# Gate and up products by Strassen's scheme, the down product over all PSUM banks, and a rearranged mixer order, in a fused encoder block

## The chip, the cores and the metric

One core of a Trainium2 chip runs the whole program. The metric is device time in microseconds of one execution, and the figure of a kernel is the median of its runs. TensorE (PE) multiplies, VectorE (DVE), ScalarE (ACT) and GpSimd (POOL) do the elementwise work, and SyncE (SP) issues nearly all transfers.

## What is computed

The block works on 512 tokens of 1024 channels in float32: a SwiGLU layer, a mixer, and a second SwiGLU layer, each with a norm ahead and a norm and a residual behind.

```python
def swiglu(x, w_gu, w_down):
    gu = x @ w_gu
    gate, up = gu[..., :D_FF], gu[..., D_FF:]
    return (jax.nn.silu(gate) * up) @ w_down

    f = swiglu(rmsnorm(x, ffn1_norm_pre), ffn1_w_gu, ffn1_w_down)
    x = x + 0.5 * rmsnorm(f, ffn1_norm_post)
    m = hybrid_mixer(rmsnorm(x, mix_norm_pre), ...)
    x = x + rmsnorm(m, mix_norm_post)
    f = swiglu(rmsnorm(x, ffn2_norm_pre), ffn2_w_gu, ffn2_w_down)
    x = x + 0.5 * rmsnorm(f, ffn2_norm_post)
```

D_FF is 2816, that is 22 blocks of 128. The mixer has a recurrence over 8 heads (solved here in chunks by small matrix products) and a causal convolution of width 31, both fed by one projection, and a shared output projection.

## The kernel before

**Three products for one.** Every large product is made from operands that are split in two: a high part, rounded to the type fp32r, and a low part, the rest. `mm3` (L118 to 125) issues three matmuls for each 128x128 block of weights: high by high, low by high, high by low. A block of weights, [128, 1024] float32 and 512 KB, is loaded by SP into a raw buffer (`wload`), cast on ACT into its high part (L97) and subtracted on DVE into its low part (L100), in `wblock`. The pool for these holds two raw, two high and two low buffers.

**Order of the work.** An engine works through its instructions in order. The order is fixed when the program is built: the framework walks the program with modelled times and, at each engine, lets the ready instruction go first that has the lowest priority number. Numbers follow the order of the program text; `tc.cur_priority` shifts them, and `after` forces one instruction behind another. The loads of `load` (L74) are chained, so they keep their order in SP's queue, and one that waits for a buffer holds those behind it. `PLAN`, a string, sets the order of the mixer's steps and how far some are put off; the `T_` strings say which PSUM tags a step uses. PSUM has eight banks, here three of tag A, three of B and two of C (D is C as well).

**An FFN** (`ffn`). `token_halves` makes the first four blocks of weights (gate and up of f = 0 and 1) on 256 tokens at a time, because the second half of the tokens is still being normed and turned (`Turn`: transposes on PE, split on ACT and DVE, L171 and L172, or L176 and L178 in the first FFN). Then f runs from 2 to 21: two blocks of weights, gate and up, each with 8 slices of the contraction, three matmuls of 512 tokens for each slice, 48 matmuls for an f. Then `tail`: silu on ACT (L294), product with up on DVE (L295), and the split of the result (L297, L298). The down product goes over the outputs in two halves of 512 columns: half 0 for k from 0 to 21, half 1 for k to 13 in the same manner, and the last eight k token block by token block, so that each of the four token blocks ends early and its norm (`Post.piece`, L244; `rs`; `add`, L251) and the next layer's norm and transposes (`between`) run beside the matmuls of the next block. `Post.piece` of half 0 runs ahead of that, for all four blocks.

**Between the stages.** The first three blocks of the mixer's projection (`LEAD`) are cast during the end of FFN 1 and go through `token_halves` as well. `w_out` makes the mixer's output projection in the same way, with `ahead` in it: it loads and casts the first four blocks of FFN 2 and loads the residual (`x2`, four tiles, from the DRAM copy `xs`). In that stage the raw weights lie in the tag "g", which has 22 buffers of 4 KB a partition. FFN 1 keeps its input `x` in SBUF until the end of its down product, and so does FFN 2 with `x2`.

## Time and profile before

| | |
|---|---|
| median of 3 runs | 1077.54 us (1077.13 to 1078.13) |
| the profiled execution's own time | 1079.54 us |
| its span, from first to last instruction | 1077.3 us |
| mean granted clock of TensorE | 0.977 |
| DMA moved | 101.27 MB, 94 GB/s |

The profile is of one execution. A duration in it is that of one instruction on its engine, and on one engine the next instruction may start before the one before it has ended, so the distance between two starts is what a busy engine takes for each. For TensorE the starts of successive matmuls are used throughout. "Idle before" is the time in which the engine stood, with what ended it behind the arrow.

### The profile page before, as it was taken

Reading aid. Unit: us, or ns where it says so; the run is one execution under the profiler, and the core shown is the slowest. Engines: PE = TensorE matmul, PEld = TensorE weight load, DVE = VectorE, ACT = ScalarE, POOL = GpSimd, SP = SyncE. Lnnn points to the kernel's source line nnn. Section 1 sums busy time; section 2 is a strip of 40 time slices with the busy share of each in tenths; the row PEclk is TensorE's granted clock in tenths of the full one; section 3 lists DMA queues with packets and bytes.
Section 4 is the critical chain, followed back from the end, with each engine's and each line's share of the span. In section 5 each row is a group of like instructions: output and inputs, shape, how many; then the busy total and the mean of one; then the engine's idle time right before and its main releaser. Section 6 shows DMA issues by size and latency. Waiting matters only on the chain.

```text
span 1077.3 us, 15404 instructions
## 1 busy us (share of the span) xinstructions
PE 1029.7 (96%) x6274; PEld 847.1 (79%) x6274; DVE 532.2 (49%) x1011; ACT 406.7 (38%) x628; POOL 151.1 (14%) x170
## 2 busy tenths in 40 slices
...
GB/s 235 64 93 99 97 98 98 98 99 98 98 98 221 52 92 60 50 80 60 89 90 21 114 81 37 162 20 85 106 84 101 94 99 97 98 98 98 98 117 78
DMA packets 52846, 101.27 MB, mean 94 GB/s; under 512 B 28584, under 2 KB 28712, under 8 KB 52776
## 3 DMA queue, kind: packets, MB, share of 16 engines
...
q10 hardware_dynamic: 864, 2.63, 0.7%
...
## 4 chain that ended last, share of the span: by engine, by line
PE 78%; DVE 11%; ACT 3%; POOL 3%; DMA 2%; issue 2%; SPq 1%; DVEq 0%; ACTq 0%
PE ps L125 25%; PE ps L121 25%; PE ps L124 25%; POOL cacc L521 3%; DVE ps L513 2%; DVE x L251 1%; ACT ms_j L132 1%; PE ps L652 1%; DVE wlo L100 1%; DVE rs_w L50 1%; DMA N<-md 1%; DVE fg L244 1%; PE ps L618 0%; ACT whi L97 0%; ACT cpr L520 0%
## 5 line engine op out<-in xcount | busy, mean ns | idle before, releaser
L121 PE MATMUL ps<-hT,whi 128*128 128x512 f32 (+1 forms) x888 | 340.3, 384 | 2.7 <-ACT hT L171 2.6
L124 PE MATMUL ps<-hT,wlo 128*128 128x512 f32 (+1 forms) x888 | 339.0, 382 | 0.7 <-DVE wlo L100 0.7
L125 PE MATMUL ps<-hT,whi 128*128 128x512 f32 (+1 forms) x888 | 338.4, 382 | 1.2 <-DVE hT L172 1.0
L100 DVE TENSOR_TENSOR wlo<-wraw,whi 128x1024 fp32r<-128x1024 f32 x141 | 175.3, 1244 | 313.9 <-ACT whi L97 313.7
L97 ACT CAST whi<-wraw 128x1024 fp32r<-128x1024 f32 x141 | 147.5, 1047 | 288.9 <-PE ps L125 168.3
L121 PEld LDWEIGHTS ps<-hT,whi 128*128 128x128 f32 x888 | 169.0, 190 | 38.7 <-ACT hT L171 3.6
L125 PEld LDWEIGHTS ps<-hT,whi 128*128 128x128 f32 x888 | 168.7, 190 | 38.1 <-issue 4.8
L124 PEld LDWEIGHTS ps<-hT,wlo 128*128 128x128 f32 x888 | 168.8, 190 | 34.0 <-DVE wlo L100 1.3
L521 POOL TENSOR_TENSOR cacc<-cacc,cpr 128x192 f32<-128x192 f32 (+2 forms) x120 | 118.5, 988 | 51.9 <-ACT cpr L520 43.7
L121 PE MATMUL ps<-whi,g 128*128 128x512 f32 x288 | 112.0, 389 | 0.0
L124 PE MATMUL ps<-whi,g 128*128 128x512 f32 x288 | 112.0, 389 | 0.0
L125 PE MATMUL ps<-wlo,g 128*128 128x512 f32 x288 | 104.4, 389 | 0.0
L294 ACT ACTIVATE sg<-ps 128x512 f32<-128x512 f32 x44 | 26.3, 598 | 166.1 <-PE ps L125 166.1
L295 DVE TENSOR_TENSOR sg<-sg,ps 128x512 f32<-128x512 f32 x44 | 30.3, 688 | 111.6 <-PE ps L125 111.6
L520 ACT ACTIVATE cpr<-gpad,vecs 128x192 f32<-128x192 f32 (+2 forms) x120 | 67.6, 574 | 36.4 <-POOL cacc L521 36.0
L154 POOL TENSOR_TENSOR fg<-x,gain 128x1024 f32<-128x1024 f32 x8 | 19.1, 2385 | 441.1 <-DVE x L251 436.5
L124 PEld LDWEIGHTS ps<-whi,g 128*128 128x128 f32 x288 | 54.1, 188 | 11.3
L125 PEld LDWEIGHTS ps<-wlo,g 128*128 128x128 f32 x288 | 54.1, 188 | 11.2
L121 PEld LDWEIGHTS ps<-whi,g 128*128 128x128 f32 x288 | 54.1, 188 | 11.1
L513 DVE SCALAR_TENSOR_TENSOR ps<-gpad,vecs,ps 128x320 f32<-128x320 f32 (+1 forms) x87 | 40.3, 464 | 1.4
L298 DVE TENSOR_TENSOR g<-sg,g 128x512 fp32r<-128x512 f32 x44 | 30.1, 685 | 1.4 <-ACT g L297 1.4
L297 ACT CAST g<-sg 128x512 fp32r<-128x512 f32 x44 | 27.0, 613 | 5.5 <-DVE sg L295 5.5
...
## 6 DMA issues: line engine op xcount, KB each, us to landing
wraw<-w SPq DMA_DIRECT2D x145, 512.0 KB, 3.6
lraw<-w SPq DMA_DIRECT2D x17, 512.0 KB, 5.1
gain<-gains ACTq DMA_DIRECT2D x5, 512.0 KB, 4.6
x<-x SPq DMA_DIRECT2D x4, 512.0 KB, 6.5
xs<-x SPq DMA_DIRECT2D x4, 512.0 KB, 2.7
x<-xs SPq DMA_DIRECT2D x4, 512.0 KB, 6.4
out<-x SPq DMA_DIRECT2D x3, 512.0 KB, 2.6
...
```

The source lines that it names most:

```text
L97: c.last_hi = nc.scalar.copy(hi, raw)
L100: c.last_lo = nc.vector.tensor_tensor(lo, raw, hi, ALU.subtract)
L121: i = nc.tensor.matmul(out, lhsT=lh, rhs=rh, start=start, stop=False)
L124: nc.tensor.matmul(out, lhsT=ll, rhs=rh, start=False, stop=False)
L125: return nc.tensor.matmul(out, lhsT=lh, rhs=rl, start=False, stop=stop)
L294: nc.scalar.activation(sg, psg, AF.Silu)
L295: nc.vector.tensor_tensor(sg, sg, psu, ALU.mult)
L297: nc.scalar.copy(g[:, 0], sg)
L298: nc.vector.tensor_tensor(g[:, 1], sg, g[:, 0], ALU.subtract)
L513: self.dve_queue(nc.vector.scalar_tensor_tensor(dst, gp[:, j : j + n], dw[:, j : j + 1], lo, ALU.mult, ALU.add), False)
L520: nc.scalar.mul(pr, gp[:, n + j : j + SEQ], dw[:, j : j + 1])
L521: self.pool_queue(nc.gpsimd.tensor_tensor(hi, hi, pr, ALU.add), j == 1)
```

## The change

- **Units.** f = 0 to 3 stay as they were. The other 18 are made in 18 `Unit`s to an FFN, by turns two gate blocks and two up blocks. A unit's product is a 2 by 2 matrix of blocks: two blocks of 128 output features, two halves of the contraction, two halves of the tokens. Strassen's scheme (in Winograd's form) makes it with seven block products instead of eight, and sums ahead of and behind them. Each product has 4 slices, three matmuls of 256 tokens each: 84 matmuls for a unit.
- **Sums ahead.** Of the weights: four sums of 512 columns on DVE, and high and low parts of 3.5 times 1024 columns (`wblock`, `dh`/`dl`, `sh`/`sl`, `a22`). Of the activations: `Combos`, once for each FFN, 14 instructions of 1024 columns on DVE and four casts on ACT, placed in the program behind f = 1 and ahead of f = 2.
- **Sums behind.** In `run`: one copy on ACT, five additions on DVE that read PSUM. Silu and product work on 1024 columns at a time.
- **Down.** `ffn_down` takes a block of 128 rows and all 1024 columns for each k, into eight accumulators in all eight banks; the last four k go token block by token block. The split of the gated product moves here. `Post.piece` of both halves runs in the token loop.
- **Buffers.** Tags with fixed counts (`SLOTS`) replace the 22 buffers of "g" and the separate pool for `x` and the gains. `sums` and `dif` have one buffer each, the sums' high and low parts one each, a22 one, the differences two. The input is loaded again during the down product; FFN 2's is first stored to `xs2`. The raw weights of `w_out` and of FFN 2's first four blocks share the two buffers of "raw2".
- **Mixer.** `PLAN`, three priority offsets (`O_PV`, `O_N`, `O_T`) and three PSUM tag strings get new values.

```diff
@@ -77,11 +77,19 @@
...
+SLOTS = {"g": 12, "s34": 4, "s12": 2, "sr": 2, "a22": 1, "sg": 2, "tmp": 2, "raw2": 2}
...
+def slot(c, shape, dt, name, tag="g"):
+    return c.gp.tile(shape, dt, name=name, tag=tag, bufs=SLOTS[tag])
@@ -271,78 +279,214 @@
...
-def preload(c, blocks, tag, raws=(), own=2, prev=None, aprev=None):
+def preload(c, blocks, tag, raws=(), own=2, prev=None, aprev=None, home="g"):
...
     for n, i in enumerate(blocks):
         hi = lo = None
         if n >= own:
-            hi = c.gp.tile([P, 1024], F32R, name="lhi", tag="g", bufs=NF)
-            lo = c.gp.tile([P, 1024], F32R, name="llo", tag="g", bufs=NF)
+            hi, lo = (slot(c, [P, 1024], F32R, name, h) for name, h in zip(("lhi", "llo"), home if len(home) == 2 else (home, home)))
         ws.append(wblock(c, i, hi, lo, raws[n] if n < len(raws) else wload(c, i, tag), prev, aprev))
     return ws
...
-def ffn(c, wbase, ws, turn, gpost, scale, finish, ahead=None):
+class Combos:
+    def __init__(self, c, ht, pool, tag):
+        nc = c.nc
+        self.ht = ht
+        self.t = pool.tile([P, 4, 2, KD // 2, 256], F32R, name="tsum", tag=tag)
+        q = lambda s, kh, th: ht[:, s, kh * 4 : kh * 4 + 4, th * 256 : th * 256 + 256]
+        d = slot(c, [P, 4, 256], F32, "td")
+        e = slot(c, [P, 4, 256], F32, "te")
+        T = slot(c, [P, 4, 256], F32, "ts")
+        def keep(n, x):
+            nc.scalar.copy(self.t[:, n, 0], x)
+            nc.vector.tensor_tensor(self.t[:, n, 1], x, self.t[:, n, 0], ALU.subtract)
+        sub = lambda o, a, b: nc.vector.tensor_tensor(o, a, b, ALU.subtract)
+        add = lambda o, a, b: nc.vector.tensor_tensor(o, a, b, ALU.add)
+        sub(d, q(0, 1, 1), q(0, 0, 1))
+        sub(e, q(1, 1, 1), q(1, 0, 1))
+        add(d, d, e)
+        keep(2, d)
+        sub(T, q(0, 0, 1), q(0, 0, 0))
+        sub(e, q(1, 0, 1), q(1, 0, 0))
+        add(T, T, e)
+        keep(0, T)
+        d = slot(c, [P, 4, 256], F32, "td")
+        sub(d, q(0, 1, 1), T)
+        add(d, d, q(1, 1, 1))
+        keep(1, d)
+        e = slot(c, [P, 4, 256], F32, "te")
+        sub(e, q(0, 1, 0), d)
+        add(e, e, q(1, 1, 0))
+        keep(3, e)
+    def t_(self, n):
+        return lambda s, k: self.t[:, n, s, k]
+    def b(self, kh, th):
+        return lambda s, k: self.ht[:, s, kh * 4 + k, th * 256 : th * 256 + 256]
+class Unit:
+    def __init__(self, c, i, cb, aprev=None):
+        self.c, self.cb = c, cb
+        nc = c.nc
+        r0, r1 = wload(c, i), wload(c, i + 1, "raw2")
+        H = slice(0, 512), slice(512, 1024)
+        sums = slot(c, [P, 1024], F32, "s12", "sr")
+        dif = slot(c, [P, 1024], F32, "s34", "sr")
+        S1, S2, S3, S4 = sums[:, H[0]], sums[:, H[1]], dif[:, H[0]], dif[:, H[1]]
+        add_eng = nc.gpsimd if POOL_ADDS else nc.vector
+        add_eng.tensor_tensor(S1, r1[:, H[0]], r1[:, H[1]], ALU.add)
+        add_eng.tensor_tensor(S3, r0[:, H[0]], r1[:, H[0]], ALU.subtract)
+        wh, wl = wblock(c, i, raw=r0, aprev=aprev)
+        nc.vector.tensor_tensor(S2, S1, r0[:, H[0]], ALU.subtract)
+        nc.vector.tensor_tensor(S4, r0[:, H[1]], S2, ALU.subtract)
+        dh, dl = slot(c, [P, 1024], F32R, "dhi", "s34"), slot(c, [P, 1024], F32R, "dlo", "s34")
+        a22 = slot(c, [P, 2, 512], F32R, "a22", "a22")
+        sh, sl = slot(c, [P, 1024], F32R, "shi", "s12"), slot(c, [P, 1024], F32R, "slo", "s12")
+        nc.scalar.copy(dh, dif)
+        nc.vector.tensor_tensor(dl, dif, dh, ALU.subtract)
+        nc.scalar.copy(sh, sums)
+        nc.vector.tensor_tensor(sl, sums, sh, ALU.subtract)
+        nc.scalar.copy(a22[:, 0], r1[:, H[1]])
+        c.last_hi = c.last_hi
+        nc.vector.tensor_tensor(a22[:, 1], r1[:, H[1]], a22[:, 0], ALU.subtract)
+        self.w = {"a11": (wh[:, H[0]], wl[:, H[0]]), "a12": (wh[:, H[1]], wl[:, H[1]]), "a22": (a22[:, 0], a22[:, 1]),
+                  "s1": (sh[:, H[0]], sl[:, H[0]]), "s2": (sh[:, H[1]], sl[:, H[1]]),
+                  "s3": (dh[:, H[0]], dl[:, H[0]]), "s4": (dh[:, H[1]], dl[:, H[1]])}
+    def mm(self, out, w, x):
+        h, l = self.w[w]
+        for k in range(4):
+            ks = slice(k * P, k * P + P)
+            mm3(self.c, out, h[:, ks], l[:, ks], x(0, k), x(1, k), k == 0, k == 3)
+    def run(self, n):
+        c, nc, cb = self.c, self.c.nc, self.cb
+        tt = nc.vector.tensor_tensor
+        pa, pb, pc, pd = (psum(c, [P, 2, 256], T_UNIT[n % 2][j]) for j in range(4))
+        u = slot(c, [P, 4, 256], F32, "u", "tmp")
+        self.mm(pa[:, 0], "a11", cb.b(0, 0))
+        self.mm(pa[:, 1], "s2", cb.t_(1))
+        nc.scalar.copy(u[:, 3], pa[:, 0])
+        tt(u[:, 0], u[:, 3], pa[:, 1], ALU.add)
+        self.mm(pb[:, 0], "s1", cb.t_(0))
+        self.mm(pb[:, 1], "s3", cb.t_(2))
+        tt(u[:, 1:3], u[:, 0:1].broadcast_to([P, 2, 256]), pb, ALU.add)
+        self.mm(pd[:, 0], "a12", cb.b(1, 0))
+        tt(u[:, 0], u[:, 3], pd[:, 0], ALU.add)
+        tt(u[:, 3], u[:, 2], pb[:, 0], ALU.add)
+        self.mm(pc[:, 0], "s4", cb.b(1, 1))
+        self.mm(pc[:, 1], "a22", cb.t_(3))
+        tt(u[:, 1:3], u[:, 1:3], pc, ALU.add)
+        return u
+T_UNIT = ("ABAC", "ABAD")
+POOL_ADDS = False
...
+def ffn_up(c, wbase, ws, turn, pool, tag):
     nc = c.nc
...
+    gs = []
+    def pair():
+        g = slot(c, [P, 2, 512], F32, "g2")
+        gs.extend([g[:, 0], g[:, 1]])
+        return g
+    pss = [psum(c, [P, 512], tag) for tag in "AAAD"]
+    token_halves(c, ws, pss, turn)
+    for f0 in range(0, LEADF, 2):
+        g = pair()
+        sg = slot(c, [P, 2, 512], F32, "sg", "sg")
...
+            if f0 == 0:
+                ps = pss[2 * f : 2 * f + 2]
+            else:
+                ps = []
+                for j in range(2):
+                    wh, wl = wblock(c, wbase + 2 * (f0 + f) + j, aprev=turn.last if f0 + f == 2 else None)
+                    ps.append(psum(c, [P, 512], "A"))
+                    for k in range(KD):
+                        mm3(c, ps[j], wh[:, k * P : k * P + P], wl[:, k * P : k * P + P], turn.ht[:, 0, k], turn.ht[:, 1, k], k == 0, k == KD - 1)
+            nc.scalar.activation(sg[:, f], ps[0], AF.Silu)
+            nc.vector.tensor_tensor(g[:, f], sg[:, f], ps[1], ALU.mult)
+        if f0 == LEADF - 4 or LEADF == 2:
+            cb = Combos(c, turn.ht, pool, tag)
+    for n in range(NF - LEADF):
+        un = Unit(c, wbase + 2 * LEADF + 2 * n, cb, aprev=turn.last if n == 0 and LEADF == 2 else None)
+        u = un.run(n)
+        if n % 2 == 0:
+            sg = slot(c, [P, 4, 256], F32, "sg", "sg")
+            nc.scalar.activation(sg, u, AF.Silu)
+        else:
+            g = pair()
+            nc.vector.tensor_tensor(g.rearrange("p a (h t) -> p (a h) t", h=2), sg, u, ALU.mult)
+    return gs
...
+NS = 4
+LEADF = 4
...
+def ffn_down(c, wbase, gs, gpost, scale, finish, xin, ahead=None):
+    nc = c.nc
+    wd = wbase + 2 * NF
+    acc = [[psum(c, [P, 512], t) for t in tt] for tt in T_DOWN]
+    def split(k, tag="g"):
+        g = slot(c, [P, 2, 512], F32R, "gh", tag)
+        nc.scalar.copy(g[:, 0], gs[k])
+        nc.vector.tensor_tensor(g[:, 1], gs[k], g[:, 0], ALU.subtract)
+        return g
+    def step(k, g, w, t, h, prev=None):
+        return mm3(c, acc[t][h], g[:, 0, t * P : t * P + P], g[:, 1, t * P : t * P + P],
+                   w[0][:, h * 512 : h * 512 + 512], w[1][:, h * 512 : h * 512 + 512], k == 0, k == NF - 1, prev)
+    for k in range(NF - NS):
+        w = wblock(c, wd + k)
+        if k >= X_AT and (k - X_AT) % 2 == 0 and (k - X_AT) // 2 < NT:
+            xin((k - X_AT) // 2)
+        g = split(k, "sg")
...
+            for h in range(2):
+                step(k, g, w, t, h)
+    big = c.gp.tile([P, NS, 2, 1024], F32R, name="wlast", tag="big")
+    last = []
+    for n in range(NS):
+        k = NF - NS + n
+        last.append((k, split(k), wblock(c, wd + k, big[:, n, 0], big[:, n, 1], wload(c, wd + k, "raw2"))))
+    posts = [Post(c, gpost, scale) for _ in range(NT)]
+    if ahead is not None:
+        ahead(None, None)
+    i = None
+    for t in range(NT):
+        for h in range(2):
+            for k, g, w in last:
+                i = step(k, g, w, t, h, i)
+            q = posts[t].piece(h * 512, acc[t][h])
+        posts[t].rs()
+        i = finish(t, posts[t], i, q)
...
+X_AT = 4
+T_DOWN = ("CC", "AA", "AB", "BB")
@@ -356,23 +500,24 @@
...
-PLAN = 'li m1 p0 c0t320/1000 m0 p1 s0@0 p2 c1t64/300 p3 c2p/600 e0@1 s1@1 k0 lg b0@0 c3t320/1500 x e1/400 O k1/400 b1 g1 g0@1 w0'
+PLAN = 'li m1 p0 m0 c0t320/1500 p1 s0@0 p2 c1t64/0 p3 e0@1 c2p/1500 k0 lg s1/400 b0@0 c3t320/1500 e1/-400 x k1/150 O b1 g1 g0@1 w0'
...
-T_COMB = ('A', 'C')
+T_COMB = ('A', 'A')
...
-O_PV = (0, 0, 0, 0)
-O_N = (-150, -150)
-O_T = (100, 0)
+O_PV = (0, 0, 40, 0)
+O_N = (0, -150)
+O_T = (-60, 0)
...
-T_ACC1 = 'CABB'
+T_ACC1 = 'CBBC'
...
-T_PRE2 = 'CB'
+T_PRE2 = 'BB'
...
+T_TURN = 'CD'
@@ -893,7 +1038,7 @@
...
-    ws = preload(c, [wbase + 4 + kb for kb in W_ORDER], RAW_WS, own=0)
+    ws = preload(c, [wbase + 4 + kb for kb in W_ORDER], "raw2", own=0)
@@ -935,27 +1080,27 @@
...
+    xs2 = c.dp.tile([SEQ, D], F32, name="xs2")
...
-            xt = c.qp.tile([P, D], F32, name="x", tag="q4")
+            xt = slot(c, [P, D], F32, "x", "s34")
             load(c, xt, A["x"][t * P : t * P + P, :])
...
-        raws += [wload(c, i, "g") for i in (2, 3)]
+        raws += [wload(c, i, "raw2") for i in (2, 3)]
@@ -966,17 +1111,19 @@
...
-        gpo, gpr = gain(c, 1, turn.last), gain(c, 2, turn.last)
+        gs = ffn_up(c, 0, ws, turn, c.gp, "big")
+        x = [slot(c, [P, D], F32, "x", "s34") for _ in range(NT)]
+        gpo, gpr = gain(c, 1), gain(c, 2)
...
-                turns.append(Turn(c, new_ht(), "CD"))
+                turns.append(Turn(c, new_ht(), T_TURN))
@@ -986,7 +1133,10 @@
...
+        def ahead(i, j):
+            lws.extend(preload(c, range(NB_FFN, NB_FFN + len(LEAD)), "raw2", home="g"))
+        ffn_down(c, 0, gs, gpo, 0.5, fin, lambda t: load(c, x[t], A["x"][t * P : t * P + P, :]), ahead)
@@ -1035,7 +1185,7 @@
...
-        turns = [Turn(c, c.gp.tile([P, 2, KD, SEQ], F32R, name="hT3", tag="ht3"), T_PRE2)]
+        turns = [Turn(c, c.gp.tile([P, 2, KD, SEQ], F32R, name="hT3", tag="big"), T_PRE2)]
@@ -1045,28 +1195,26 @@
...
+            nc.sync.dma_start(xs2[t * P : t * P + P, :], x2[t])
             return between(tn, t, i, x2[t], gpr, post.fg)
...
         def ahead(i, j):
-            def f2():
-                lws.extend(preload(c, range(B2, B2 + 4), RAW_F2, own=OWN_F2, prev=j, aprev=i))
-            if not X_FIRST:
-                f2()
+            lws.extend(preload(c, range(B2, B2 + 4), "raw2", own=OWN_F2, prev=j, aprev=i, home=("tmp", "sg")))
             for t in range(NT):
-                x2.append(c.qp.tile([P, D], F32, name="x", tag="q4"))
+                x2.append(slot(c, [P, D], F32, "x", "s34"))
                 load(c, x2[t], xs[t * P : t * P + P, :])
-            if X_FIRST:
-                f2()
...
+        gs = ffn_up(c, B2, lws, turns[0], hp, "ht")
         gpo2 = gain(c, 5)
+        x3 = [slot(c, [P, D], F32, "x", "s34") for _ in range(NT)]
...
-                post.add(x2[t], x2[t], sl)
-                nc.sync.dma_start(O["out"][t * P : t * P + P, sl], x2[t][:, sl])
-        ffn(c, B2, lws, turns[0], gpo2, 0.5, fin2)
+                post.add(x3[t], x3[t], sl)
+                nc.sync.dma_start(O["out"][t * P : t * P + P, sl], x3[t][:, sl])
+        ffn_down(c, B2, gs, gpo2, 0.5, fin2, lambda t: load(c, x3[t], xs2[t * P : t * P + P, :]))
```

## Rows read from the trace of the kernel before

**Rows 1.** Page, part 1: busy time, share of the span and instructions of each engine.
```profile
PE 1029.7 (96%) x6274; PEld 847.1 (79%) x6274; DVE 532.2 (49%) x1011; ACT 406.7 (38%) x628; POOL 151.1 (14%) x170
```

**Rows 2.** Stretches: us, busy time and instructions by engine, granted TensorE clock, DMA share, GB/s.
```profile
38.70:256.40 217.70, 217.70 (x963) 180.26 (x962) 73.69 (x79) 61.17 (x79) 0.00 (x0) 1.00 0.31 96
...
256.40:300.00 43.60, 43.60 (x194) 36.12 (x193) 11.09 (x10) 9.11 (x10) 0.00 (x0) 1.00 0.32 101
...
420.00:620.00 200.00, 174.01 (x1948) 130.41 (x1946) 166.66 (x369) 114.40 (x193) 109.72 (x110) 0.93 0.29 72
...
620.00:683.00 63.00, 55.27 (x519) 44.50 (x519) 52.76 (x136) 37.08 (x74) 13.81 (x24) 0.91 0.28 98
...
733.00:950.60 217.60, 217.60 (x962) 180.17 (x961) 73.74 (x80) 61.45 (x80) 0.00 (x0) 1.00 0.32 96
```

**Rows 3.** Groups by shape, 60.68 to 256.4 us: count, busy us, mean ns, idle before.
```profile
L121 PE MATMUL ps<-hT,whi 128*128 128x512 f32 x288 | 112.0, 389 | 0.0
...
L100 DVE TENSOR_TENSOR wlo<-wraw,whi 128x1024 fp32r<-128x1024 f32 x36 | 44.1, 1226 | 81.9 <-ACT whi L97 81.9
...
L97 ACT CAST whi<-wraw 128x1024 fp32r<-128x1024 f32 x36 | 37.7, 1047 | 69.2 <-PE ps L125 69.2
...
L295 DVE TENSOR_TENSOR sg<-sg,ps 128x512 f32<-128x512 f32 x18 | 12.4, 688 | 46.6 <-PE ps L125 46.6
...
L298 DVE TENSOR_TENSOR g<-sg,g 128x512 fp32r<-128x512 f32 x18 | 12.3, 684 | 0.0
...
L297 ACT CAST g<-sg 128x512 fp32r<-128x512 f32 x18 | 11.0, 613 | 0.0
...
L294 ACT ACTIVATE sg<-ps 128x512 f32<-128x512 f32 x18 | 10.8, 598 | 70.7 <-PE ps L125 70.7
```

**Rows 4.** Timeline, VectorE, gate and up of FFN 1: start us, duration us, engine, line.
```profile
60.68 0.69 DVE L295 TENSOR_TENSOR sg<-sg,ps 128x512 f32<-128x512 f32 x1 [2.59 <-PE ps L125]
...
61.77 1.23 DVE L100 TENSOR_TENSOR wlo<-wraw,whi 128x1024 fp32r<-128x1024 f32 x1 [0.40 <-ACT whi L97]
...
62.91 0.69 DVE L298 TENSOR_TENSOR g<-sg,g 128x512 fp32r<-128x512 f32 x1
...
71.56 0.69 DVE L295 TENSOR_TENSOR sg<-sg,ps 128x512 f32<-128x512 f32 x1 [2.59 <-PE ps L125]
```

**Rows 5.** Timeline, TensorE, token halves of FFN 1: first and last of 23 matmuls.
```profile
23.08 0.28 PE L124 MATMUL ps<-hT,llo 128*128 128x256 f32 x1
...
25.71 0.28 PE L125 MATMUL ps<-hT,lhi 128*128 128x256 f32 x1
```

**Rows 6.** Timeline, VectorE, end of FFN 1: one 512-column instruction and the next.
```profile
380.71 0.68 DVE L172 TENSOR_TENSOR hT<-ps,hT 128x512 fp32r<-128x512 f32 x1
...
381.31 0.20 DVE L53 SCALAR_TENSOR_TENSOR rs_w<-rs_y,ms_s 128x1 f32<-128x1 f32 x1
```

**Rows 7.** Groups by shape, whole run: the smallest two-operand instruction on VectorE.
```profile
L790 DVE TENSOR_TENSOR SV<-ps,LC 64x128 f32<-64x128 f32 x28 | 8.0, 286 | 0.5
```

**Rows 8.** Timeline, VectorE, start of FFN 1 and of FFN 2.
```profile
27.64 2.16 DVE L178 SCALAR_TENSOR_TENSOR hT<-ps,gcol,hT 128x128 fp32r<-128x128 f32 x8 [1.58 <-ACT hT L176]
...
34.46 1.23 DVE L100 TENSOR_TENSOR wlo<-wraw,whi 128x1024 fp32r<-128x1024 f32 x1 [4.66 <-ACT whi L97]
...
720.87 1.29 DVE L172 TENSOR_TENSOR hT<-ps,hT 128x512 fp32r<-128x512 f32 x2 [2.45 <-ACT hT L171]
...
732.78 0.69 DVE L295 TENSOR_TENSOR sg<-sg,ps 128x512 f32<-128x512 f32 x1 [1.72 <-PE ps L125]
```

**Rows 9.** Stretch around the first matmuls of FFN 2: columns as in rows 2.
```profile
705.00:710.00 5.00, 4.57 (x25) 4.36 (x26) 4.16 (x14) 2.17 (x3) 0.59 (x1) 0.70 0.33 105
```

**Rows 10.** Timelines, VectorE: last casts ahead of FFN 2, first residual add of w_out.
```profile
684.26 2.35 DVE L100 TENSOR_TENSOR llo<-lraw,lhi 128x1024 fp32r<-128x1024 f32 x2
...
688.47 1.28 DVE L251 SCALAR_TENSOR_TENSOR x<-fg,rs_y,x 128x1024 f32<-128x1024 f32 x1
```

**Rows 11.** Page, part 6: DMA issues, KB each, median us from issue to landing.
```profile
x<-xs SPq DMA_DIRECT2D x4, 512.0 KB, 6.4
```

More of the change, by code (lines that the diff above doesn't have):

```diff
@@ L83, in wload @@
     else:
-        raw = c.gp.tile([P, 1024], F32, name="lraw", tag=tag, bufs=NF if tag == "g" else NRAW2)
+        raw = slot(c, [P, 1024], F32, "lraw", tag)
     load(c, raw, c.A["w"][i])
@@ L197, in diag @@
         for t in range(2):
-            dg = c.gp.tile([P, P], F32, name="dg", tag="g", bufs=NF)
+            dg = slot(c, [P, P], F32, "dg")
             self.put(x[t], None, dg)
@@ L254, in gain @@
 def gain(c, i, prev=None):
-    g = c.qp.tile([P, D], F32, name="gain", tag="q4")
+    g = slot(c, [P, D], F32, "gain", "s12")
     i = c.nc.scalar.dma_start(g, c.A["gains"][i : i + 1, :].broadcast_to([P, D]))
```

71 lines of the change are left out of this document (7 added, 64 removed).

## The prediction, made before the changed kernel ran

> **What bounds the kernel now.** I read the busy shares first: TensorE is busy in 96% of the span, VectorE in 49%, ScalarE in 38% [rows 1]. A share is a mean, so the stretches come next [rows 2]. In the gate and up products of either FFN TensorE is busy for the whole stretch, 217.70 of 217.70 us and 217.60 of 217.60, at full granted clock, while VectorE is busy for a third of it. The down product that follows is as dense. So in the FFNs, some 675 of 1077 us (435 in these two stretches, and 2 x 528 matmuls of the down products at 0.2267), time is the number of matmuls times the distance of their starts, and only fewer or shorter matmuls, or a new wait, can change it. The mixer is another matter: between 420 and 683 us TensorE stands for 34 us in all and VectorE is busy for 219 of 263 us. What is cut from VectorE's work elsewhere is worth nothing; what is added to it in the FFNs has some 140 us of room in each gate and up stretch.
>
> **TensorE's gain.** In the stretch of gate and up everything repeats with f [rows 3]: two weight casts, two subtractions, and no wait on TensorE. One f takes from 60.68 to 71.56 us, the starts of two successive products with up: 10.88 us, or 0.2267 for each of 48 matmuls of 512 columns [rows 4]. A unit has 84 matmuls of 256 columns. Such matmuls, each with new weights, run today in the token halves, 22 starts in 2.63 us: 0.1195 each [rows 5]. That is more than half of 0.2267, so Strassen's eighth is partly lost to a fixed cost: a unit takes 84 x 0.1195 = 10.04 us and saves 0.84, not 1.36. With 36 units: **-30.2 us**.
>
> The Trainium skill (TensorE: Matmul & The Clock Gate, Back-to-back issue gap) tables 262 cycles for 256 columns and 518 for 512; by it, at 2.4 GHz, I estimate 1.19 us saved per unit and 42.9 in all. The rows above give less for the shorter matmul, and the measurement decides.
>
> **VectorE's new load.** This decides whether the 30.2 arrive. Two 1024-column subtractions start 1.14 us apart where the first is shown with 1.23 [rows 4]; after a 512-column one the next starts at 0.60 [rows 6]. For 256 columns I interpolate durations between 0.286 (128 columns) [rows 7] and 0.688 (512) [rows 3]: 0.42, or 0.34 from start to start. Per unit: three low parts of 1024 (3.42), four weight sums and a22's low part (5 x 0.60 = 3.00), behind the products three additions of 256 (1.02) and two of 512 (1.20), half a product of 1024 (0.57). Sum 9.21 us, in 10.04 of TensorE's. ScalarE: three and a half casts (3 x 1.047 + 0.6), a copy and half a silu (some 0.9), 4.6 us [rows 3]. So TensorE still sets the pace, but the cover on VectorE falls from 7 us to 0.8 per unit, and weights can be made only one unit ahead, since sums and their parts have one buffer. Where VectorE waits for ScalarE or for a product, that cover is soon used. Bounds: 0, and all of the 0.84. I take 0.1 per unit, **+3.6**, near the lower end, because with 0.8 to spare a handover or two of this length is absorbed.
>
> **Combos.** Fourteen 1024-column instructions, 16 us of VectorE, can start once the tokens are turned, at 29.8 us in FFN 1 (27.64 + 2.16) and 722.2 in FFN 2 [rows 8]. The subtraction for f = 2, today at 34.46, stands behind them in the program. TensorE wants it when the token halves end, near 38.9 and 733.0: one matmul behind 38.70, where the stretch of full-width matmuls begins [rows 2], and behind 732.78, where the product with up marks the end of the halves in FFN 2 [rows 8]. If all but the last of the fourteen go first, with two products of 0.60 between, it is ready at 29.8 + 14.8 + 1.2 + 1.2 = 47.0, 8.1 late, and at 739.4 in FFN 2, 6.4 late. If it slips into a pause, while a combination waits for its cast (1.047 against 1.14 of the work beside it: nearly a tie), it is not late at all. Bounds 0 and 14.5; I take 2.5 for each FFN, **+5**, since the tie has to fall badly for the full price.
>
> **Down.** The matmuls stay 528 of 512 columns. Casts and split take 1.14 + 0.60 on VectorE and 1.05 + 0.61 on ScalarE for each k, under 24 x 0.2267 = 5.44 of TensorE: no cost, also with another microsecond on either. The first accumulators use banks free since earlier in the last unit, the split of k = 0 needs only an old result. The token loop gains one `piece` per block, some 0.7 us of VectorE; in FFN 1 the last may show, in FFN 2 the extra half lies 2.7 us ahead of the end. **+0.7**, bounds 0 and 3. Twelve more 512 KB transfers lie in stretches with DMA at a third.
>
> **w_out into FFN 2.** The raw blocks now share two buffers, and the four `x2` loads stand in SP's queue behind FFN 2's raws, the last of which must wait for casts that today begin at 684.26 [rows 10]. A load of `x2` lands 6.4 us after issue [rows 11]: with an issue at 684.3, 690.7 at the earliest, where the first residual add starts today at 688.47 [rows 10]. Everything behind it on VectorE (rsqrt, next `piece`, transposes' split) moves, partly into pauses. TensorE feels it as an added wait ahead of the token halves, where a pause of 1.2 and one of 0.4 us already go with a granted clock of 0.70 over 5 us [rows 9], between the levels of 1.2 and 2.4 GHz. Bounds 0 and 6; I take **+2**.
>
> **Mixer.** The order of steps, conv's put-off and solve's offsets change, no amount of work. It can gain no more than the 34 us in which TensorE stands [rows 2], or lose as much; a wait of the kind seen there is some 6 us. With no row for either sign: 0, and 5 either way in the range.
>
> **Sum.** -30.2 + 3.6 + 5 + 0.7 + 2 = -18.9. About 0.2%, some 2 us, is what a measurement of this kernel can tell from no change; the sum is nine times that. The profiled execution took 1079.54, its span 1077.3 and 2.2 around it; the sum makes it 1060.6. The median of the runs is 2.0 below that execution, so I forecast 1077.5 - 18.9 = 1058.6, rounded to **1058**. Its own range is 1046 (no cost at all) to 1067.
>
> **Rivals.**
> *Combos hold VectorE in full.* For it: program order puts them ahead. Against: the pauses. 14.5 in place of 5, and some 3 more at the lower clock that follows a pause [rows 9]: 1058 + 12.5 = 1070.5. Chance 0.16.
>
> *VectorE becomes the bound*: each instruction occupies it for its whole shown duration. The same list then costs 3 x 1.226 + 5 x 0.684 + 3 x 0.42 + 2 x 0.688 + 0.61 = 10.35 us per unit, and 36 x (10.88 - 10.35) = 19.1 is all that is gained; with 7.7 of the other costs, 1066. Against it: the starts at 1.14 and 0.60 [rows 4, 6]. Chance 0.10. The Trainium skill (VectorE: DVE Perf Modes, The DRAIN you can't avoid) says that the next operation does not start until the pipe has emptied, which is this rival; the starts here come 0.08 earlier than the shown ends, so by the trace it is unlikely.
>
> *Slower: the sums' single buffers close a loop.* If VectorE's queue has the low parts of the next unit (2 x 1.14) behind the last addition (0.60) and the pair's product (0.57) of this one, TensorE, which needs them 1.43 us into the next unit, waits 3.45 - 1.43 = 2.0 us per unit: 12.06 instead of 10.88, 36 x 1.2 = +43, with the 7.7 about 1128; half of that stall gives 1092. It decides from 0.84 - 7.7 / 36 = 0.63 us of stall per unit. For it: one buffer each, 0.8 us of cover. Against: the product with s1 is done at 3/7 of a unit, so its buffer is free 5.7 us before the end. Chance 0.14, with the mixer's bad end.
>
> **Numbers.** Forecast 0.60, rivals 0.16, 0.10, 0.14. The first three are faster, less 0.03 for ends that come near nothing: faster 0.83, same 0.04, slower 0.13. The range of 8 in 10 takes in the first two rivals: 1046 to 1074.
>
> **What would show it.** TensorE's starts in units at 0.1195, 10.04 us per unit, with idle near zero; VectorE at about 9.2 of 10 us busy by starts; the first subtraction of f = 2 before or after the end of the token halves; in FFN 2 the first `x` add later than the matmuls it follows; mixer time from first to last step within 5 us of before. Idle of TensorE on low parts (`slo`, `dlo`) in every unit would make the prediction wrong, and so would a mixer that is 10 us longer or shorter.

## The result, and the profile after

The changed kernel takes **1060.89 us** (median of 4 runs, 1059.17 to 1061.34), the kernel before 1077.42 beside it: ratio 0.9843, interval 0.9826 to 0.986. It is 16.5 us faster; 1058 was forecast, in a range of 1046 to 1074. The profiled execution took 1061.24, its span is 1059.5.

The busy shares of the changed kernel, to be read against [rows 1]:

```profile
PE 1004.6 (95%) x7570; PEld 887.1 (84%) x7570; DVE 785.6 (74%) x1417; ACT 487.4 (46%) x726; POOL 151.9 (14%) x170
```

TensorE has more instructions and less time; VectorE went from 49% to 74%. The stretches of the changed kernel, columns as in [rows 2]: f = 2 and 3 beside the Combos, the units of FFN 1, the units of FFN 2:

```profile
38.23:60.10 21.87, 21.87 (x99) 18.11 (x98) 21.53 (x23) 9.82 (x11) 0.00 (x0) 1.00 0.35 121
60.10:241.45 181.35, 181.35 (x1513) 181.35 (x1512) 166.29 (x240) 82.60 (x100) 0.00 (x0) 1.00 0.34 108
751.00:932.00 181.00, 181.00 (x1510) 181.00 (x1509) 166.27 (x240) 82.59 (x100) 0.00 (x0) 1.00 0.34 108
```

In all three TensorE is busy from end to end at full granted clock. A unit takes 181.35 / 18 = 10.08 us of TensorE and 166.29 / 18 = 9.24 us of VectorE; forecast were 10.04 and 9.21. TensorE's timeline inside a unit has the starts of successive matmuls of 256 columns 0.12 apart, as in [rows 5]:

```profile
99.85 0.28 PE L133 MATMUL ps<-tsum,a 128*128 128x256 f32 x1
99.97 0.28 PE L129 MATMUL ps<-tsum,a 128*128 128x256 f32 x1
```

The groups by shape in the units' stretch (count, busy us, mean ns, idle before) have VectorE's three sizes; the 0.415 us for 256 columns is what I had interpolated as 0.42:

```profile
L359 DVE TENSOR_TENSOR dlo<-s,dhi 128x1024 fp32r<-128x1024 f32 x18 | 21.9, 1218 | 0.0
L354 DVE TENSOR_TENSOR s<-wraw,s 128x512 f32<-128x512 f32 x17 | 11.6, 685 | 0.0
L384 DVE TENSOR_TENSOR u<-u,ps 128x256 f32<-128x256 f32 x18 | 7.5, 415 | 2.0 <-ACT u L383 2.0
```

To find where the rest of the time went, I put the same milestones of both traces side by side (us into the span; the last column is the change in the length of the stage that ends there):

| milestone | before | after | stage |
|---|---|---|---|
| first full-width matmul of FFN 1 | 38.70 | 38.23 | -0.5 |
| first matmul of its down product | 256.3 | 241.5 | -14.4 |
| last split of FFN 1's turned tokens | 392.07 | 380.09 | +2.9 |
| last split of the mixer's output | 670.70 | 659.97 | +1.3 |
| start of w_out's last residual add | 707.98 | 706.40 | +9.1 |
| last split of FFN 2's turned tokens | 722.16 | 718.84 | -1.7 |
| end | 1077.3 | 1059.5 | -14.5 |

The two gate and up products give 28.9 us. Between them 11.6 us are lost (2.9 + 1.3 + 9.1 - 1.7), most of it in the stage of w_out.

**The Combos.** VectorE's timeline from the start of FFN 1:

```profile
33.99 1.23 DVE L108 TENSOR_TENSOR wlo<-wraw,whi 128x1024 fp32r<-128x1024 f32 x1 [4.66 <-ACT whi L105]
35.14 0.68 DVE L427 TENSOR_TENSOR g<-sg,ps 128x512 f32<-128x512 f32 x1
35.73 1.22 DVE L309 TENSOR_TENSOR td<-hT 128x1024 f32<-128x1024 f32 x1
...
39.14 1.22 DVE L108 TENSOR_TENSOR wlo<-wraw,whi 128x1024 fp32r<-128x1024 f32 x1
...
45.54 1.22 DVE L108 TENSOR_TENSOR wlo<-wraw,whi 128x1024 fp32r<-128x1024 f32 x1
...
59.76 1.22 DVE L307 TENSOR_TENSOR tsum<-te,tsum 128x1024 fp32r<-128x1024 f32 x1
```

The subtraction for f = 2 runs at 33.99, where it ran before [rows 8]: ahead of the Combos, not behind them. VectorE stood idle for 4.66 us ahead of it, with the tokens turned, so the Combos are not first in its queue. They begin behind the first gated product (35.14), and the low parts for f = 2 and 3 stand between them. They last until 61, and TensorE never waits.

**The token loop of FFN 1.** The four residual adds on VectorE's timeline, in the changed kernel:

```profile
347.76 1.28 DVE L259 SCALAR_TENSOR_TENSOR x<-fg,rs_y,x 128x1024 f32<-128x1024 f32 x1
354.33 1.28 DVE L259 SCALAR_TENSOR_TENSOR x<-fg,rs_y,x 128x1024 f32<-128x1024 f32 x1
361.96 1.28 DVE L259 SCALAR_TENSOR_TENSOR x<-fg,rs_y,x 128x1024 f32<-128x1024 f32 x1
369.55 1.28 DVE L259 SCALAR_TENSOR_TENSOR x<-fg,rs_y,x 128x1024 f32<-128x1024 f32 x1
```

Between the first two of them VectorE waits for the mean square of `x`, and then runs the pieces of the next block's two halves (L252):

```profile
350.33 0.15 DVE L165 TENSOR_SCALAR ms_s<-ms_s 128x1 f32<-128x1 f32 x1 [1.28 <-ACT ms_j L140]
...
351.59 0.68 DVE L252 SCALAR_TENSOR_TENSOR fg<-ps,gain 128x512 f32<-128x512 f32 x1
...
352.33 0.68 DVE L252 SCALAR_TENSOR_TENSOR fg<-ps,gain 128x512 f32<-128x512 f32 x1
```

In the kernel before there is one piece between the first two adds (L244; the first half's had run ahead of the loop):

```profile
362.55 1.28 DVE L251 SCALAR_TENSOR_TENSOR x<-fg,rs_y,x 128x1024 f32<-128x1024 f32 x1
...
366.49 0.68 DVE L244 SCALAR_TENSOR_TENSOR fg<-ps,gain 128x512 f32<-128x512 f32 x1
...
368.44 1.28 DVE L251 SCALAR_TENSOR_TENSOR x<-fg,rs_y,x 128x1024 f32<-128x1024 f32 x1
```

The adds are 6.57, 7.63 and 7.59 us apart; before they were 5.89, 6.93 and 6.89 (starts at 362.55, 368.44, 375.37 and 382.26). Each block has 0.7 us more. From 350.33 to the next add VectorE works without a pause, so the second piece lies in the chain between two adds; with the small instruction ahead of it (L250) it takes 0.66 us from start to start (351.53 to 352.19).

**w_out.** The chain of waits of the changed kernel around the first residual add (start, duration, what):

```profile
665.85 4.49 DMA lraw<-w
...
672.70 4.21 DMA lraw<-w
...
679.33 3.52 DMA lraw<-w
...
682.88 1.06 ACT lhi L105
...
685.26 0.60 DVE fg L252
...
687.05 1.29 DVE x L259
```

Before, no transfer stood there: ScalarE cast the raw blocks one behind the other (its timeline in the kernel before, the four of FFN 2 following from 680.91 on):

```profile
670.22 3.90 ACT L97 CAST lhi<-lraw 128x1024 fp32r<-128x1024 f32 x4
```

Now eight raw blocks go through two buffers, and three times a subtraction frees a buffer, a transfer fills it, a cast empties it. The add follows its rsqrt at once; the loads of `x2` (issued at 679.71) are not in the chain.

### The profile page after: what moved, and what is told of

The parts are those of the page before. It is cut to its first block, busy times and chain, and to the rows that moved or that the text cites. A ratio compares the mean times of both kernels' runs of the same rounds, so it can differ in the third digit from the quotient of the medians.

```text
span 1059.5 us, 18641 instructions
## 1 busy us (share of the span) xinstructions
PE 1004.6 (95%) x7570; PEld 887.1 (84%) x7570; DVE 785.6 (74%) x1417; ACT 487.4 (46%) x726; POOL 151.9 (14%) x170
## 4 chain that ended last, share of the span: by engine, by line
PE 73%; DVE 12%; ACT 4%; POOL 4%; DMA 4%; issue 2%; SPq 0%; DVEq 0%; ACTq 0%; POOLq 0%
PE ps L129 23%; PE ps L133 23%; PE ps L132 23%; POOL cacc L666 4%; DVE ps L658 2%; DMA lraw<-w 1%; DVE wlo L108 1%; DVE x L259 1%; PE ps L797 1%; ACT cpr L665 1%; ACT whi L105 1%; DMA N<-md 1%; DVE rs_w L50 1%; ACT ms_j L140 1%; DVE E L745 1%
## 5 line engine op out<-in xcount | busy, mean ns | idle before, releaser
L129 PE MATMUL ps<-hT,whi 128*128 128x256 f32 (+1 forms) x600 | 196.9, 330 | 4.5 <-ACT hT L179 4.2
L132 PE MATMUL ps<-hT,wlo 128*128 128x256 f32 (+1 forms) x600 | 195.8, 328 | 1.3 <-DVE wlo L108 1.0
L133 PE MATMUL ps<-hT,whi 128*128 128x256 f32 (+1 forms) x600 | 195.1, 327 | 0.4 <-DVE hT L186 0.2
L129 PEld LDWEIGHTS ps<-hT,whi 128*128 128x128 f32 x600 | 116.0, 193 | 18.5 <-ACT hT L179 5.1
L133 PEld LDWEIGHTS ps<-hT,whi 128*128 128x128 f32 x600 | 115.3, 193 | 13.7 <-issue 4.0
L132 PE MATMUL ps<-whi,gh 128*128 128x512 f32 x288 | 112.0, 389 | 0.0
L133 PE MATMUL ps<-wlo,gh 128*128 128x512 f32 x288 | 112.0, 389 | 0.0
L132 PE MATMUL ps<-tsum,slo 128*128 128x256 f32 x288 | 80.0, 283 | 0.0
L133 PE MATMUL ps<-tsum,shi 128*128 128x256 f32 x288 | 80.0, 283 | 0.0
L129 PE MATMUL ps<-tsum,shi 128*128 128x256 f32 x288 | 76.3, 283 | 0.0
L129 PE MATMUL ps<-whi,gh 128*128 128x512 f32 x288 | 71.5, 389 | 0.0
L132 PEld LDWEIGHTS ps<-whi,gh 128*128 128x128 f32 x288 | 54.1, 188 | 11.2
L129 PEld LDWEIGHTS ps<-whi,gh 128*128 128x128 f32 x288 | 53.9, 188 | 11.1
L132 PEld LDWEIGHTS ps<-tsum,slo 128*128 128x128 f32 x288 | 55.3, 192 | 0.0
L133 PEld LDWEIGHTS ps<-tsum,shi 128*128 128x128 f32 x288 | 55.3, 192 | 0.0
```

The costliest lines, as they stand in the source:

```text
L129: i = nc.tensor.matmul(out, lhsT=lh, rhs=rh, start=start, stop=False)
L132: nc.tensor.matmul(out, lhsT=ll, rhs=rh, start=False, stop=False)
L133: return nc.tensor.matmul(out, lhsT=lh, rhs=rl, start=False, stop=stop)
```

## The experiments

**Four raw buffers for w_out and FFN 2.**

```diff
-    ws = preload(c, [...], "raw2", own=0)
+    ws = preload(c, [...], ("raw2", "raw2", "sr", "sr"), own=0)
-    lws.extend(preload(c, range(B2, B2 + 4), "raw2", ...))
+    lws.extend(preload(c, range(B2, B2 + 4), ("raw2", "raw2", "sr", "sr"), ...))
```

> Four raw buffers instead of two for the eight blocks loaded in w_out (the two of sr stand idle there). Theory, the loads queue on two buffers: the third and fourth block of w_out are cast before TensorE needs them, its wait of 3.4 us ahead of a transpose and the one of 1.2 us vanish, the stage from the mixer's last split to the last residual add falls from 46.4 us (37.3 in the kernel before) to 37 to 39, and the time to 1052 to 1054. Rival, the new PSUM tags of w_out and of FFN 2's turn make the slip: the stage stays at 45 to 47 and the time within 2 us of 1060.9.

Measured: 1053.43 us (1051.99 to 1054.1), ratio 0.9764 [0.9748, 0.978]. The stage from the last mix split to the last add is 40.0 us, a little above the 37 to 39 expected (the combinations below show why), and ScalarE's casts are again without a wait for a transfer (its timeline):

```profile
660.77 3.90 ACT L105 CAST lhi<-lraw 128x1024 fp32r<-128x1024 f32 x4
...
671.57 1.99 ACT L105 CAST whi<-lraw 128x1024 fp32r<-128x1024 f32 x2
673.46 1.99 ACT L105 CAST lhi<-lraw 128x1024 fp32r<-128x1024 f32 x2
```

The order of instructions on VectorE, ScalarE and GpSimd is that of the changed kernel, so the 7.5 us (8.5 by the two ratios to the kernel before) are the price of two buffers instead of four; 6.5 of them lie in this stage.

**The loads of `x2` first.** My prediction had blamed these loads.

```diff
+            for t in range(NT):
+                x2.append(slot(c, [P, D], F32, "x", "s34"))
+                load(c, x2[t], xs[t * P : t * P + P, :])
             lws.extend(preload(c, range(B2, B2 + 4), "raw2", ...))
-            for t in range(NT):
-                x2.append(slot(c, [P, D], F32, "x", "s34"))
-                load(c, x2[t], xs[t * P : t * P + P, :])
```

> The four loads of x2 stand ahead of FFN 2's raw blocks in SP's queue; nothing else is changed. Prediction's step (the loads of x2, held behind raw blocks that wait for casts, make w_out's residual adds late): with the loads ahead the stage from the last mix split to the last add falls from 46.4 to 38 to 40 us, and the time to 1053 to 1055. Theory from the chain of waits of after (the residual add waits for its rsqrt, which stands behind casts of raw blocks that went round through two buffers; the loads of x2 are in time as it is): the stage stays 46 within 1, the time 1061 within 1.5.

Measured: 1062.61 (1061.57 to 1063.97), ratio 0.9855 [0.9842, 0.9869], not to be told from the changed kernel. The prediction's reason is refuted; the stage even grew to 49.4 us, as the second round trip, now beside 2 MB of `x2`, took 6.37 us instead of 4.21. The chain of this kernel:

```profile
665.59 4.51 DMA lraw<-w
...
672.45 6.37 DMA lraw<-w
...
681.23 4.37 DMA lraw<-w
```

**Four buffers for w_out's blocks alone.**

```diff
-    ws = preload(c, [...], "raw2", own=0)
+    ws = preload(c, [...], ("raw2", "raw2", "sr", "sr"), own=0)
```

> Four buffers for w_out's four raw blocks alone; FFN 2's four still go through two. The chain of after has three round trips (subtraction frees a buffer, transfer, cast): 4.49, 4.21 and 3.52 us. Theory: the first two go, because FFN 2's first two raw blocks can then be fetched while w_out's matmuls run, the third stays: 7.5 - 3.5 = 4 us gained, 1057, between 1056 and 1058.5, the stage 42 to 43 us. Rivals: it is all in w_out's own blocks (1053.4, as with four buffers for both, stage 40); or all in FFN 2's blocks (1061, stage 46).

Measured: 1058.26 (1058.0 to 1060.48), ratio 0.982 [0.9806, 0.9833]. The time is as expected, but for another reason: the stage is 45.95 us, 0.5 less than in the changed kernel, and the remaining 2 us or so are in the mixer stage (276.5 against 279.9), with an unchanged order on VectorE, ScalarE and GpSimd. So my count of round trips was wrong and the second rival right for the stage. ScalarE's timeline shows why:

```profile
659.70 3.90 ACT L105 CAST lhi<-lraw 128x1024 fp32r<-128x1024 f32 x4
...
670.50 1.99 ACT L105 CAST whi<-lraw 128x1024 fp32r<-128x1024 f32 x2
676.34 1.05 ACT L105 CAST lhi<-lraw 128x1024 fp32r<-128x1024 f32 x1 [3.86 <-DMA lraw<-w]
679.78 1.05 ACT L105 CAST lhi<-lraw 128x1024 fp32r<-128x1024 f32 x1 [2.39 <-DMA lraw<-w]
```

w_out's four casts are together now, but FFN 2's first two come only behind the Squares of w_out's products, at 670.50, and the third and fourth block can be fetched only then, 5.80 us in the chain, beside `x2`. FFN 2's own two buffers are enough to lose nearly all of it.

**The mixer settings of before, in the changed kernel** (`PLAN`, `T_COMB`, `O_PV`, `O_N`, `O_T`).

```diff
-O_PV = (0, 0, 40, 0)
+O_PV = (0, 0, 0, 0)
...
```

> The changed kernel with the mixer's order, offsets and combine tags of before. Theory, the rearrangement is worth little either way (FFN 1's last split to the mixer's last split takes 279.9 us after, 278.6 before): time 1058 to 1064. Rival, the old order no longer fits behind the new FFN and the rearrangement is worth something: 1066 or more. Rival, it costs something: 1057 or less.

Measured: 1058.63 (1057.43 to 1059.58), ratio 0.9813 [0.9793, 0.9832]: within the 1058 to 1064 of the theory, and about 2 to 3 us faster than with the new settings, with an interval that still overlaps the other's. The mixer stage is 279.4 us against 279.9; what differs is the stage from the last mix split to the last add, 44.1 against 46.4.

**The new settings alone, in the kernel before.**

```diff
-O_PV = (0, 0, 0, 0)
+O_PV = (0, 0, 40, 0)
...
```

> The kernel before with the new mixer order, offsets and combine tags alone. Theory, no gain in the order itself: 1075 to 1081. Rival, part of the 16.5 us is the mixer's own: 1072 or less.

Measured: 1079.27, ratio 1.0006 [0.9995, 1.0016]. No difference: the mixer stage is 1.6 us shorter (277.1), the one behind it 2.8 longer (40.0), and the turn behind that 1.5 shorter (12.7 against 14.2). So the rearranged order brings nothing in the time by itself.

**The Combos first.** The subtraction for f = 2 is made to wait for the thirteenth of the fourteen.

```diff
-wh, wl = wblock(c, ..., aprev=...)
+wh, wl = wblock(c, ..., prev=cb.end if (f0 + f, j) == (2, 0) else None, aprev=...)
```

> The first low part for f = 2 is forced behind thirteen of the fourteen Combos instructions on VectorE, in both FFNs. Theory, the order on VectorE alone decides whether Combos cost something: the product of f = 0 (35.1 us) still goes first, then 13 x 1.14 and another product, so the low part comes near 51 us where TensorE wants it at 38.5, a wait of 11 to 13 us in FFN 1 and much the same in FFN 2, in all 20 to 26 us: 1080 to 1088, slower than the kernel before. Rival, TensorE finds other work or the wait is caught up later: under 1068.

Measured: 1094.81 in one run, 33.9 above the changed kernel and above the 1080 to 1088 of the theory. The first rival of the prediction, made true, costs not 17.5 us (14.5 of waits and 3 of clock) but 34. TensorE's waits in this run (total, times, longest):

```profile
PE ps L132 <- DVE wlo L108: 28.5, 3, 15.0
```

Stretches around the first one, columns as in [rows 2]:

```profile
38.00:43.00 5.00, 0.99 (x7) 0.55 (x5) 5.00 (x6) 1.04 (x1) 0.00 (x0) 0.89 0.00 0
43.00:48.00 5.00, 0.00 (x0) 0.00 (x0) 4.93 (x5) 1.70 (x2) 0.00 (x0) 0.50 0.00 0
...
53.00:58.00 5.00, 5.00 (x18) 3.97 (x17) 1.25 (x2) 0.00 (x0) 0.00 (x0) 0.75 0.70 210
58.00:63.00 5.00, 5.00 (x24) 4.14 (x23) 1.23 (x1) 1.53 (x2) 0.00 (x0) 1.00 0.00 0
```

28.5 us are waits, 13.0 of them in FFN 1 and 15.0 in FFN 2. Behind each of these two, the granted clock is still at its lower level for a part of the next 5 us (0.75), in which 18 matmuls start instead of 24: 6 x 0.2267 = 1.4 us more, twice. The two gate and up products take 218.2 and 220.7 us against 203.2, so 4.0 us come on top of the waits. The waits are longer than the prediction had them because the Combos start late. VectorE's timeline in FFN 1:

```profile
34.55 0.69 DVE L427 TENSOR_TENSOR g<-sg,ps 128x512 f32<-128x512 f32 x1 [5.09 <-PE ps L133]
...
50.76 2.35 DVE L108 TENSOR_TENSOR wlo<-wraw,whi 128x1024 fp32r<-128x1024 f32 x2
```

Here too they stand behind the first gated product, for which VectorE waits 5.09 us with the tokens turned (8.41 us in FFN 2).

**No units.** `LEADF = 22` makes all f plain; the Combos are left out, buffers, down product and mixer settings stay.

```diff
-LEADF = 4
+LEADF = 22
...
-        if f0 == LEADF - 4 or LEADF == 2:
-            cb = Combos(c, turn.ht, pool, tag)
```

> Every pair of gate and up is the plain product of 48 matmuls of 512 columns again, and the Combos are left out; the down product over eight banks, the tags of the buffers and the mixer order stay the changed ones. Theory (each of 36 units saves 0.81 us, the Combos cost nothing, and the down and buffer side of the change takes 12 to 13 us back): gate and up take 217.7 us per FFN again, and the time is 1060.9 + 29 = 1090, between 1086 and 1093, so some 1% slower than the kernel before; the FFN 1 token loop keeps its periods of 7.6 us and the w_out stage its 46. Rival (what was lost at the token loop and at w_out comes from the units, through VectorE's load or the loads they shift): without them the time falls back to 1077, within 3.

Measured: 1091.31 (1088.09 to 1092.7), ratio 1.0111 [1.0085, 1.0136]: 30.4 above the changed kernel, 12.4 above the one before. The token loop's adds are 6.56, 7.64 and 7.59 apart and the w_out stage is 46.25 us, as in the changed kernel. So these two losses belong to the rest of the change, not to the units. Gate and up take 42.90 to 260.5, 217.6 us as before. This kernel's first full-width matmul is 4.2 us later than before, which I have not followed.

**The next block's first piece earlier.** Matmuls and `piece` of block t + 1, half 0, ahead of `finish(t)`:

```diff
...
         posts[t].rs()
+        if t + 1 < NT and ahead is not None:
+            i, _ = half(t + 1, 0, i)
         i = finish(t, posts[t], i, q)
...
```

> In the token loop of FFN 1 the matmuls of the next block's first half and their piece stand ahead of this block's residual add and norm in the program; no work is added or left out. Theory (the second Square stands in the chain add, mean square, Square, piece, rsqrt, add only because of its place in the order): the first half's Square runs while ScalarE is idle, the period of the residual adds falls from 7.6 to 6.9 us, TensorE's 2.85 us wait on the transposed tokens gets shorter or goes, and the time is 1058 to 1059 (2 to 3 us less). Rival (the period is set by VectorE's extra piece, or by the matmuls): periods of 7.6 and 1061 within 1; a third possibility is that the first half's accumulators, ready earlier, change nothing and the later turn of a block costs a new wait of TensorE: 1061 to 1064.

Measured: 1065.45 (1063.15 to 1067.97), ratio 0.9878 [0.9856, 0.99]. In the loop the gain came, and more than was expected: the adds are 5.78, 5.80 and 7.00 us apart, the last turned tokens come 3.6 us earlier (376.45), and TensorE's wait of 2.9 is down to 0.5. The residual adds of this kernel on VectorE's timeline:

```profile
348.06 1.28 DVE L259 SCALAR_TENSOR_TENSOR x<-fg,rs_y,x 128x1024 f32<-128x1024 f32 x1
353.84 1.29 DVE L259 SCALAR_TENSOR_TENSOR x<-fg,rs_y,x 128x1024 f32<-128x1024 f32 x1
359.64 1.28 DVE L259 SCALAR_TENSOR_TENSOR x<-fg,rs_y,x 128x1024 f32<-128x1024 f32 x1
366.64 1.28 DVE L259 SCALAR_TENSOR_TENSOR x<-fg,rs_y,x 128x1024 f32<-128x1024 f32 x1
```

The theory had named ScalarE's Square as what stands in the chain; in the changed kernel's trace it is VectorE's piece, as the rival had it. The edit moves both, and the matmuls ahead of them. VectorE now runs the first half's piece in its pause for the mean square of `x`:

```profile
349.32 0.68 DVE L252 SCALAR_TENSOR_TENSOR fg<-ps,gain 128x512 f32<-128x512 f32 x1
350.62 0.15 DVE L165 TENSOR_SCALAR ms_s<-ms_s 128x1 f32<-128x1 f32 x1 [0.61 <-ACT ms_j L140]
```

But the mixer stage is 285.4 us instead of 279.9, and the median is 4.6 us higher, with intervals that just touch; the combinations repeat it with intervals that don't. None of the three expectations had that. The order in which the build places the mixer's instructions on TensorE, VectorE and ScalarE came out quite another one.

**Combinations.** Both raw-buffer edits with the old mixer settings, then with the earlier piece as well.

> The raw blocks of w_out and of FFN 2's first loads in four buffers (as in the first run), and the mixer settings of before (as in the second). Theory (two separate losses, one behind the mixer, one within it): the gains of 7.5 and 2.3 us add up, 1051, between 1050 and 1052.5. Rival (the mixer setting's gain sits in the same wait behind the mixer): 1053.4 within 0.8, as with the raw buffers alone.

> The edits of the two runs named before and the earlier piece of FFN 1's token loop together. Theory (three separate losses): 1048 to 1049.5. Rival (a token loop that ends earlier is taken back in the mixer, whose start waits for its own loads): the time without the earlier piece, 1050 to 1052.

Measured: 1052.28 (1050.84 to 1053.46), ratio 0.9755 [0.9738, 0.9771], and 1056.12 (1056.03 to 1058.4), ratio 0.9796 [0.9781, 0.9812]. In the time the first can't be told from the raw buffers alone (0.9764), so neither theory nor rival is settled by it. The stages say more: the w_out stage is 37.1 us, against 40.0 with the raw buffers alone and 37.3 before, while the mixer stage is 278.3 against 277.0. In all three pairs of old and new settings (before, changed, four raw buffers) the new ones make w_out's stage longer, by 2.8, 2.3 and 2.8 us, and change the mixer's by -1.6, +0.5 and -1.3. The 9.1 us lost at w_out are thus some 6.3 of the raw buffers and 2.8 of the settings, and nothing is left for the new PSUM tags of w_out. The earlier piece costs some 4 us again, outside both expectations, and its mixer stage is 285.3 us again (278.3 without it). The first of the two, or the raw buffers alone, is the best version found; both beat both kernels.

**More load on VectorE in the units.** A low part made twice, in one half and in full.

```diff
+        nc.vector.tensor_tensor(dl[:, H[0]], S3, dh[:, H[0]], ALU.subtract)
```
```diff
+        nc.vector.tensor_tensor(dl, dif, dh, ALU.subtract)
```

> Each unit of both FFNs has one 512-column subtraction more on VectorE (a half of a low part is made twice), 0.60 us from start to start. Theory (VectorE's time counts by starts, 9.24 of 10.08 us per unit): 9.84, still under TensorE's 10.08; the units' stretch in FFN 1 stays 181.4 us within 1 and VectorE is at 98%. Rival (handovers need the rest of the cover): 0.1 to 0.5 us per unit, a stretch of 183 to 190.

> Each unit of both FFNs has one 1024-column subtraction more on VectorE (a low part is made twice), 1.14 us from start to start. Theory: 9.24 + 1.14 = 10.38 us per unit, 0.30 over TensorE's; VectorE becomes the bound, the units' stretch in FFN 1 grows from 181.4 to 187 and the time by 11 to 1072. Rival (with VectorE at its limit each late low part stops TensorE and is followed by a lower clock): more than 0.8 us per unit, a stretch over 196 and a time over 1090.

Measured, one run each: 1061.88 and 1074.21. The first down matmul starts at 241.6 and at 246.4, so the units' stretch is 181.4 and 186.2 us, 10.08 and 10.35 for a unit. The stretch of the changed kernel's units, with the half more:

```profile
60.10:241.45 181.35, 181.35 (x1513) 181.31 (x1512) 173.97 (x254) 81.14 (x100) 0.00 (x0) 1.00 0.33 106
```

And the same stretch with the whole subtraction more:

```profile
60.10:241.45 181.35, 179.34 (x1479) 177.68 (x1477) 180.85 (x252) 80.31 (x97) 0.00 (x0) 1.00 0.32 102
```

With the half more (9.84 us per unit by the sum of starts) VectorE is busy for 173.97 of 181.35 us, 96% where 98% were expected, and TensorE loses nothing inside the units; one wait of 1.0 us, for the last addition, appears where the down product begins. With 10.38 VectorE is busy for 180.85 of 181.35 and sets the pace, at its own sum; the granted clock stays at 1.00, so the rival's second half did not come. Of the 13.3 us in the time 9.6 are the two stretches, and 2.2 are a mixer stage of 282.0 us, with another order on VectorE.

## Why the prediction was right, and where its terms were not

The total was near for the right main reason, and near also by luck: the Combos, the handovers, the turn and the start were priced 9.5 us too high, the token loop, w_out and the mixer's settings 10.6 too low, and these nearly cancelled. Terms in us, against the milestones (the sum of the measured ones is the difference of the two profiled spans; the medians are 16.5 apart):

| term | forecast | measured |
|---|---|---|
| units with handovers | -30.2 + 3.6 | -28.9 |
| Combos | +5 | 0 |
| down and token loop | +0.7 | +2.9 |
| w_out, raw buffers | +2 | +6.3 |
| mixer, and w_out by its settings | 0 | +1.3 + 2.8 |
| turn behind w_out | 0 | -1.7 |
| start | 0 | -0.5 |
| sum | -18.9 | -17.8 |

The lower end of the sum's own range is a slip: with no cost at all, 1077.5 - 30.2 gives 1047.3 and not 1046. The forecast had no term for the turn behind w_out: it is 12.4 us in the changed kernel with the new or the old mixer settings and 14.2 in the kernel before, and why stays open.

**TensorE's gain held.** 10.88 - 10.08 = 0.80 per unit against 0.84, because a matmul of 256 columns costs 0.12, more than half of 0.2267. The 42.9 us that I had estimated by the Trainium skill (TensorE: Matmul & The Clock Gate, Back-to-back issue gap) did not come; the rows of the kernel before were the better price.

**VectorE's load held, its handovers were priced too high.** 9.24 us by starts against 9.21; with 0.8 us to spare no handover is lost, and the half subtraction shows that 0.24 (by the sum of starts) is still enough. "VectorE becomes the bound" is refuted in the form it had: by shown durations the list is 10.35 us, and the unit takes 10.08. The Trainium skill (VectorE: DVE Perf Modes, The DRAIN you can't avoid) has the next operation wait for the pipe to empty, and adds that one which is not held starts earlier. The starts in these runs come 0.08 us before the shown ends, and it is the starts that add up to the limit (10.38 by the sum of starts with the whole subtraction, 10.35 measured). The single buffers closed no loop: no wait of TensorE stands in either FFN's gate and up.

**The Combos step failed** at "all but the last of the fourteen go first". The program's order was not the order on the engine: the Combos did not start when the tokens were turned, at 29.3, but behind the subtraction at 33.99 and a product at 35.14. The forced order shows that the reason was sound and the price too low: waits of 13.0 and 15.0 us against 8.1 and 6.4, because there too the Combos began some 5 and 8 us later than the sum had them; the clock, priced at 3, took 4.0.

**Token loop: the size was off.** The engine was right, the extra `piece` on VectorE, but I took it as 0.7 us in all, as if the last block's alone would show. It stands in the chain between two residual adds, so it costs 0.7 for every block: 3 x 0.7 between the first and last add, and 0.7 in the turns behind (10.5 us against 9.8). Upper bound 3, measured 2.9; the run with the piece earlier, whose stage is 134.7 us against 135.8 in the kernel before, shows that it costs nothing in another place of the order.

**w_out: right buffers, wrong victim, wrong size.** I followed the loads of `x2` behind the raw blocks in SP's queue, with a bound of 6. They were in time. The late ones were the casts themselves: three round trips of 4.49, 4.21 and 3.52 us through two buffers, where four buffers have none. The sum of such trips should have been the upper bound. With four buffers for both sets 7.5 us of the time come back (6.5 in this stage); with four for w_out's set alone the stage hardly moves.

**Mixer.** The +1.3 is no more than the spread of this stage, 276.5 to 279.9 us in four kernels whose order on VectorE is the same (the changed one, four raw buffers for both or for w_out, `x2` first). With the same settings it takes 275.3 us without units and 282.0 with the whole subtraction more, where the build's order in the mixer came out differently. The settings' cost, 2.8, falls behind the mixer, where I had not looked for it: the first Square of w_out's products starts 9.7 us behind the last mix split with them (668.20, four raw buffers), 6.6 with the old ones (665.89, four raw buffers; 677.32, before). Part of this is a shift of the milestone: over the mixer and w_out together the new settings cost 1.2 us in the kernel before, 2.8 in the changed one and 1.5 with four raw buffers. It is inside the 5 us either way. The 6 us that I named for a wait in the mixer have no row; TensorE's longest between 420 and 683 us of the kernel before is 4.8. Why the mixer grows by 5.5 and 7.0 us when FFN 1's tokens are turned 3.6 and 4.6 us earlier stays open: the new order on the engines is seen, but which step in it is the late one was not tried.
